# Nine small tiles instead of ten: every large tile moves down by 32 bytes

## The chip, the cores and the metric

The kernel runs on one core of a Trainium2 chip. The metric is the device time of one execution in microseconds (us). Before the change the median of three runs is 1848.85 us, from 1848.84 to 1849.08.

The core has five engines that work side by side: PE (the matrix engine; its weight loads are shown apart, as PEld), DVE (vector), ACT (scalar), POOL (general) and SP (which here issues most of the transfers). Operands lie in an on-chip memory of 128 partitions; an address in this text is a byte offset within a partition and is the same in all 128.

## The reference, cut to what matters

One layer of a streaming encoder on 256 tokens of width 2048, all in float32:

```
x = x + 0.5 * swiglu(rms_norm(x, ffn1_norm), w_gate, w_up, w_down)    # hidden width 5632
h = rms_norm(x, mix_norm);  [u | q | k | v] = h @ w_in                # 4 x 1024 columns
y_ssm = s5_mixer(u)                                                   # diagonal state space, then a gated 1024x1024 product
y_sb  = stick_breaking_attention(rms_norm(q), rms_norm(k), v)         # 8 heads of 128
x = x + concat(rms_norm(y_ssm), rms_norm(y_sb)) @ w_out
x = x + 0.5 * swiglu(rms_norm(x, ffn2_norm), ...)                     # the same again, other weights
gate = sigmoid(rms_norm(x, ple_norm) @ w_ple_gate)
x = x + rms_norm((p @ w_ple_proj) * gate, ple_post_norm)
```

Nearly all arithmetic lies in the products of 256 rows with large weight matrices.

## The kernel before, in words

A product of two float32 matrices is made of three products of a shorter type (`fp32r` in the rows, float32 bits that PE takes in one pass): each operand is split into a part `hi`, a copy rounded to that type, and a rest `lo`; then `hi*hi`, `lo*hi` and `hi*lo` are summed in an accumulator. ACT writes `hi` (line 181), DVE writes `lo` by a subtraction (line 184), and PE runs the three products (lines 323, 324 and 328 in `gemm_half`; lines 495, 496 and 498 in `Seven.product`, which does the feed-forward products with seven block products in place of eight). In each of these the moving operand is a slice of 512 columns of a weight tile (`whi`, `wlo`, or in a second ring `shi`, `slo`), 2048 bytes in each partition, and the stationary operand is a slice of 128 columns of an activation tile (`nhi`, `nlo`, `hhi`, `hlo`), 512 bytes in each partition. Some products are narrower: the gated product of the state-space part (lines 1384, 1388, 1393) has a moving operand of 256 columns, and the attention (lines 1249 to 1295) works with 256 and 512 columns.

Weights come by SP's queue as `raw` tiles of 1 MB (line 313), five buffers deep; `whi` and `wlo` have four buffers each. Where the second ring is there, `weight_pair` (line 284) takes the next pair from it or from the first by a turn of seven, `i % 7 % 2`. The change leaves that turn as it is.

All tiles come from pools, and a pool's tiles are laid one behind the other in the partition. First come a scratch of 1024 bytes for transfers, four small constants, and the pool `const` (`ident`, `ones`, `late_r`, `ident_r`, `tri_r`, `all_r` of 512 bytes each, then `gains` and `rho4`). Then comes the pool `small` with tiles of 8 float32 values, 32 bytes, named `sm`; they hold sums of squares, roots and the like. Behind `small` stand the pools of the large tiles: `wts` (`raw`, `whi`, `wlo`), `act` (`nhi` and so on), `com`, and the pools of the single phases. So the size of `small` sets where every large tile begins, while the constants in front of it don't depend on it.

A tile of `small` is taken by `small()` (line 82); the pool hands its buffers out in turn. A new tile in a buffer waits until the last use of the tile that had this buffer before. The order of instructions on each engine follows from the program's text with the generators that `step()` advances after each half chunk of a product; addresses play no part in it.

Of the kernel before, what the change touches and what calls it, by code (L numbers as in the profile page):

```python
# [33 lines left out]
def layer_kernel(ctx: ExitStack, tc: tile.TileContext, a: dict, shapes: dict, out: bass.AP):  # L34
# [15 lines left out]
    assert TT == 2 and NP == 64 and HC == 16 and DH == P and NC == 64 and SW == NH * DH  # L50

    cpool = ctx.enter_context(tc.tile_pool(name="const", bufs=1))
    smp = ctx.enter_context(tc.tile_pool(name="small", bufs=10))
    wp = ctx.enter_context(tc.tile_pool(name="wts", bufs=4))
    actp = ctx.enter_context(tc.tile_pool(name="act", bufs=1))
    comp = ctx.enter_context(tc.tile_pool(name="com", bufs=1))
# [1620 lines left out]
```

## Time and profile before

| what | value |
|---|---|
| median of three runs | 1848.85 us |
| the profiled execution's own time | 1850.29 us |
| its span, first to last instruction | 1848.5 us |
| PE busy | 1836.6 us, 99% of the span |
| DVE busy | 1462.7 us, 79% |
| ACT busy | 1019.6 us, 55% |
| POOL busy | 62.1 us, 3% |
| granted clock of PE, mean | 0.998 |

The profiled execution took 1.44 us more than the median of the runs, and 1.8 us of its time lie outside the span. A row of a timeline gives the start within the span and the time that the instruction took, both in microseconds, then engine, source line, operation, `out<-in` and how many equal instructions the row merges. The time that a matmul takes includes the run through the array, which overlaps with the next matmul; what a matmul costs in a dense stream is the distance from its start to the next one's start.

### The profile page before, as it was taken

Reading aid. Unit: us, or ns where it says so; the run is one execution under the profiler, and the core shown is the slowest. Engines: PE = TensorE matmul, PEld = TensorE weight load, DVE = VectorE, ACT = ScalarE, POOL = GpSimd, SP = SyncE. Lnnn points to the kernel's source line nnn. Section 1 sums busy time; section 2 is a strip of 40 time slices with the busy share of each in tenths; the row PEclk is TensorE's granted clock in tenths of the full one; section 3 lists DMA queues with packets and bytes.
Section 4 is the critical chain, followed back from the end, with each engine's and each line's share of the span. In section 5 each row is a group of like instructions: output and inputs, shape, how many; then the busy total and the mean of one; then the engine's idle time right before and its main releaser. Section 6 shows DMA issues by size and latency. Waiting matters only on the chain. (4 is left out here: it accounts for less than half of the span.)

```text
span 1848.5 us, 23966 instructions
## 1 busy us (share of the span) xinstructions
PE 1836.6 (99%) x9032; PEld 1519.8 (82%) x9032; DVE 1462.7 (79%) x1718; ACT 1019.6 (55%) x1187; POOL 62.1 (3%) x108
## 2 busy tenths in 40 slices
PE   9999999999999999999999999999999999999998
PEld 7888887888888888888897888888888888888887
DVE  8967664999987975687566799989898998797655
ACT  7444443555565655365685465555555645565554
POOL 0011000000000000010021000000000000000000
PEclk9999999999999999999999999999999999999999
DMA  9888867567657566675636776675656585656563
GB/s 331 286 270 281 251 213 219 182 228 239 227 189 249 191 231 206 192 263 166 212 142 215 219 272 210 227 239 190 205 182 227 198 269 185 247 183 232 180 220 125
DMA packets 232307, 406.36 MB, mean 220 GB/s; under 512 B 26784, under 2 KB 50720, under 8 KB 231904
## 3 DMA queue, kind: packets, MB, share of 16 engines
q1 hardware_dynamic: 227824, 392.81, 63.5%
q0 software_dynamic: 3648, 10.62, 1.8%
q8 instruction: 70, 1.15, 0.3%
q10 hardware_dynamic: 720, 1.41, 0.2%
q14 instruction: 45, 0.37, 0.1%
HBM read 373.46 MB, written 11.93 MB: 208 GB/s over the span
## 5 line engine op out<-in xcount | busy, mean ns | idle before, releaser
L184 DVE TENSOR_TENSOR wlo<-raw,whi 128x1024 fp32r<-128x1024 f32 x473 | 573.2, 1224 | 214.1 <-ACT whi L181 206.5
L181 ACT CAST whi<-raw 128x1024 fp32r<-128x1024 f32 x473 | 491.4, 1050 | 398.3 <-PE acc L324 258.0
L323 PE MATMUL acc<-whi,nhi 128*128 128x512 f32 x1112 | 436.8, 393 | 1.9 <-ACT whi L181 1.6
L324 PE MATMUL acc<-whi,nlo 128*128 128x512 f32 x1112 | 433.7, 390 | 0.0
L328 PE MATMUL acc<-wlo,nhi 128*128 128x512 f32 x1112 | 304.4, 390 | 0.4 <-DVE wlo L184 0.4
L323 PEld LDWEIGHTS acc<-whi,nhi 128*128 128x128 f32 x1112 | 209.2, 188 | 47.9 <-ACT whi L181 3.0
L328 PEld LDWEIGHTS acc<-wlo,nhi 128*128 128x128 f32 x1112 | 208.8, 188 | 44.6 <-DVE wlo L184 1.2
L324 PEld LDWEIGHTS acc<-whi,nlo 128*128 128x128 f32 x1112 | 209.4, 188 | 42.4
L184 DVE TENSOR_TENSOR slo<-raw,shi 128x1024 fp32r<-128x1024 f32 x166 | 202.5, 1220 | 43.8 <-ACT shi L181 43.6
L181 ACT CAST shi<-raw 128x1024 fp32r<-128x1024 f32 x166 | 174.3, 1051 | 113.4 <-PE acc L324 32.7
L181 ACT CAST whi<-sum 128x1024 fp32r<-128x1024 f32 x61 | 64.2, 1052 | 96.1 <-DVE sum L502 80.8
L181 ACT CAST shi<-sum 128x1024 fp32r<-128x1024 f32 x47 | 49.5, 1052 | 74.4 <-DVE sum L502 62.4
L324 PE MATMUL acc<-whi,hlo 128*128 128x512 f32 x216 | 84.1, 389 | 0.0
L323 PE MATMUL acc<-whi,hhi 128*128 128x512 f32 x216 | 84.1, 389 | 0.0
L324 PE MATMUL aux<-whi,hlo 128*128 128x512 f32 x200 | 78.0, 390 | 0.8 <-DVE hlo L184 0.8
L323 PE MATMUL aux<-whi,hhi 128*128 128x512 f32 x200 | 77.8, 389 | 0.0
L184 DVE TENSOR_TENSOR wlo<-sum,whi 128x1024 fp32r<-128x1024 f32 x61 | 74.6, 1222 | 1.9 <-ACT whi L181 1.2
L184 DVE TENSOR_TENSOR hlo<-hT,hhi 128x1024 fp32r<-128x1024 f32 x56 | 68.3, 1219 | 4.8 <-ACT hhi L181 4.5
L502 DVE TENSOR_TENSOR sum<-sum,raw 128x1024 f32<-128x1024 f32 x54 | 66.0, 1222 | 1.0
L181 ACT CAST hhi<-hT 128x1024 fp32r<-128x1024 f32 x56 | 58.6, 1047 | 13.8 <-PE aux L328 11.7
L328 PE MATMUL acc<-wlo,hhi 128*128 128x512 f32 x216 | 65.7, 390 | 0.2 <-DVE wlo L184 0.2
L324 PE MATMUL acc<-shi,hlo 128*128 128x512 f32 x160 | 62.3, 389 | 0.0
(373 smaller groups left out, 3016.9 us busy)
## 6 DMA issues: line engine op xcount, KB each, us to landing
raw<-in_ffn_w_up SPq DMA_DIRECT2D x88, 1024.0 KB, 5.9
raw<-in_ffn_w_down SPq DMA_DIRECT2D x88, 1024.0 KB, 5.1
raw<-in_ffn_w_gate SPq DMA_DIRECT2D x86, 1024.0 KB, 7.1
raw<-in_w_in SPq DMA_DIRECT2D x32, 1024.0 KB, 5.9
raw<-in_w_out SPq DMA_DIRECT2D x16, 1024.0 KB, 5.3
raw<-in_w_ple_gate SPq DMA_DIRECT2D x16, 1024.0 KB, 5.4
hT<-mid SPq DMA_DIRECT2D x160, 64.0 KB, 4.2
h<-mid SPq DMA_DIRECT2D x176, 32.0 KB, 2.8
```

The costliest lines, as they stand in the source:

```text
L181: copy = nc.scalar.copy(hi, src)
L184: nc.vector.tensor_tensor(out=lo, in0=src, in1=hi.bitcast(F32), op=ALU.subtract)
L323: nc.tensor.matmul(ps[t], lhsT=lh, rhs=hi[:, j, cols], start=start and j == 0, stop=False)
L324: nc.tensor.matmul(ps[t], lhsT=ll, rhs=hi[:, j, cols], start=False, stop=False)
L328: nc.tensor.matmul(ps[t], lhsT=lh, rhs=lo[:, j, cols], start=False, stop=stop and j == 1)
L502: nc.vector.tensor_tensor(out=t, in0=x, in1=y, op=ALU.add)
```

## The change

The pool of small tiles has nine buffers instead of ten:

```diff
-    smp = ctx.enter_context(tc.tile_pool(name="small", bufs=10))
+    smp = ctx.enter_context(tc.tile_pool(name="small", bufs=9))
```

The pool shrinks from 320 to 288 bytes, so every tile behind it begins 32 bytes lower. The first `raw` tile began at byte 6112, which is 32 above a multiple of 64; it now begins at 6080, a multiple of 64 (and 64 above a multiple of 128). All other large tiles have sizes that are multiples of 64 and move in the same way: `whi` from 47072 to 47040, `nhi` from 79840 to 79808, and so on. Counted over the built programs, 7990 of the 7998 `fp32r` matmuls had a moving operand that began 32 above a multiple of 64 and 7956 a stationary one; after the change none has. The others read constants: the moving operand `late_r` at line 1249, and the stationary operands `ident_r`, `tri_r` and `all_r` at lines 1249, 1288 to 1295 and 1571, began at multiples of 128 before and still do.

The order of the instructions is the same on all five engines. The small tiles fall on other buffers of their pool. Of all the waits in the program a single one is changed: POOL's instruction at line 1564, near the end, writes to a small tile whose buffer had before been last used by an ACT instruction of the last gate block (line 1495); it now waits for a much earlier ACT instruction (line 598).

## The prediction

> **What bounds the kernel now.** I read the busy times first, then the slices, then what PE waited for, then the distances between matmul starts.
>
> ```profile
> PE 1836.6 (99%) x9032; PEld 1519.8 (82%) x9032; DVE 1462.7 (79%) x1718; ACT 1019.6 (55%) x1187; POOL 62.1 (3%) x108
> ```
>
> PE is busy from end to end. DVE, the next, has 1848.5 - 1462.7 = 386 us to spare. The slices show whether that holds in each stage:
>
> ```profile
> PE   9999999999999999999999999999999999999998
> DVE  8967664999987975687566799989898998797655
> ```
>
> PE is full in all forty. DVE is nearly full in some (slices 8 to 11, most of 24 to 33), so a faster PE would meet DVE there. A busy PE could still be one that waits within its rows, so next comes the list of PE's own waits, all of it:
>
> ```profile
> PE acc L328 <- DVE slo L184: 2.2, 1, 2.2
> PE acc L323 <- ACT whi L181: 1.6, 2, 1.1
> PE aux L248 <- POOL ones L125: 1.1, 1, 1.1
> PE aux L324 <- DVE hlo L184: 0.8, 1, 0.8
> PE acc L328 <- DVE wlo L184: 0.6, 3, 0.2
> PE aux L495 <- ACT whi L181: 0.3, 1, 0.3
> PE acc L323 <- ACT whi L273: 0.2, 1, 0.2
> ```
>
> They come to 6.8 us. Whatever the change does for DVE, ACT or transfers cannot bring more than about that. What is left is PE's own rate. In the chain of work that ended last, six rows of line 328, four matmuls each, come at one distance near the end; the first and the last of the six are
>
> ```profile
> 1743.20 0.91 PE acc L328 x4
> ...
> 1756.80 0.91 PE acc L328 x4
> ```
>
> Between two of them lie twelve matmuls of 512 columns (four of line 323, four of 324, four of 328), so 60 matmuls in 13.60 us: 226.7 ns each. The number of them, from the table of one stretch over the whole span for line 323 and then for line 495 (PE busy and its count stand third and fourth):
>
> ```profile
> 0.00:1848.50 1848.50, 863.87 (x2210) 415.39 (x2210) 1.00 0.66 220
> 0.00:1848.50 1848.50, 147.31 (x378) 70.98 (x378) 1.00 0.66 220
> ```
>
> Lines 324 and 328 have the same count as 323, and 496 and 498 that of 495: 3 x 2210 + 3 x 378 = 7764, twelve of which have 256 columns; with 18 more at lines 1288 and 1571 there are 7770 of 512 columns. 7770 x 226.7 ns = 1761 us of the 1848.5. So each nanosecond on a wide matmul is 7.8 us of the kernel, and 0.5 ns is 0.2%, about what a measurement of this kernel can tell from no change.
>
> The 226.7 ns are not all columns. The gated product has moving operands of 256 columns, fourteen starts from the first of these rows to the last:
>
> ```profile
> 933.21 0.28 PE L1384 MATMUL acc<-hhi,whi 128*128 128x256 f32 x1
> ...
> 934.89 0.28 PE L1384 MATMUL acc<-hhi,whi 128*128 128x256 f32 x1
> ```
>
> 1.68 us / 14 = 120 ns. 256 columns more cost 226.7 - 120 = 106.7 ns, so 512 columns are 213.3 ns and **13.3 ns are a fixed cost of each matmul**: 7770 x 13.3 ns = 104 us. The question is whether this fixed cost has to do with operands that begin 32 bytes above a multiple of 64.
>
> **The change part by part.**
>
> *The start of the moving operand.* One place of the kernel has had it aligned all along: line 1249 in the attention reads `late_r`, a constant at a multiple of 128, with the stationary `ident_r`, also at a multiple of 128. Two of them follow each other; the first and the last time:
>
> ```profile
> 893.28 0.40 PE L1249 MATMUL aux<-late_r,ident_r 128*128 128x256 f32 x2
> 893.51 0.38 PE L1255 MATMUL aux<-q,k 128*128 128x256 f32 x1
> ...
> 938.96 0.40 PE L1249 MATMUL aux<-late_r,ident_r 128*128 128x256 f32 x2
> 939.20 0.59 PE L1255 MATMUL aux<-q,k 128*128 128x256 f32 x2
> ```
>
> From the first start to the start behind the pair: 0.23 and 0.24 us for two, 0.47 / 4 = 117.5 ns each. Nearby stand matmuls of the same width whose moving operands `sph` and `spl` begin 32 above a multiple of 64:
>
> ```profile
> 915.93 0.39 PE L1288 MATMUL aux<-sph,tri_r 128*128 128x512 f32 x1
> 916.16 0.28 PE L1291 MATMUL aux<-sph,all_r 128*128 128x256 f32 x1
> 916.28 0.29 PE L1295 MATMUL aux<-sph,tri_r 128*128 128x256 f32 x1
> 916.40 0.39 PE L1288 MATMUL aux<-spl,tri_r 128*128 128x512 f32 x1
> 916.64 0.28 PE L1291 MATMUL aux<-spl,all_r 128*128 128x256 f32 x1
> 916.76 0.28 PE L1295 MATMUL aux<-spl,tri_r 128*128 128x256 f32 x1
> 916.87 0.40 PE L323 MATMUL acc<-whi,nhi 128*128 128x512 f32 x1
> 917.11 0.39 PE L324 MATMUL acc<-whi,nlo 128*128 128x512 f32 x1
> ```
>
> 916.16 to 916.40 and 916.64 to 916.87: 0.47 / 4 = 117.5 ns. Aligned and unaligned cost the same to the resolution of the rows, some 3 ns. An aligned matmul without the fixed cost would have shown 106.7 ns, a pair 0.21 us. So I take 0 for this part. The comparison is not quite clean: `late_r` is read as the same 128 columns twice, and these are four-fold samples at half width amid a disturbed stream. I keep both ends below.
>
> *The start of the stationary operand.* Weight loads in two rows, with `ident_r` aligned in the first (shortest, median and longest time in ns) and `nhi` unaligned in the second (188 is its mean):
>
> ```profile
> L1249 PEld LDWEIGHTS aux<-late_r,ident_r x8: 187/188/192, 893.0 to 939.0; 128*128 128x128 f32 x8
> L323 PEld LDWEIGHTS acc<-whi,nhi 128*128 128x128 f32 x1112 | 209.2, 188 | 47.9 <-ACT whi L181 3.0
> ```
>
> 188 ns each. I take 0. The end on the slow side comes from line 1288 above, 512 columns with an aligned stationary operand: 916.40 to 916.64 is 0.24 us, 13 ns more than 226.7. But line 323, unaligned, is followed in that same place at the same distance (916.87 to 917.11), so the place is slow, not the alignment.
>
> *DVE, ACT and transfers.* Their operands move too. ACT wrote a constant of 128 columns once from an unaligned tile (`h`) and once from an aligned one (`ones`):
>
> ```profile
> L133 ACT ACTIVATE tri_r<-h x1: 312/312/312, 54.1 to 54.1; 128x128 fp32r<-128x128 f32 x1
> L136 ACT ACTIVATE all_r<-ones x1: 307/307/307, 19.0 to 19.0; 128x128 fp32r<-128x128 f32 x1
> ```
>
> 5 ns, or nothing: one sample each. No row shows DVE or a transfer on aligned large tiles, so they are bounded by who waits for them. If they get faster, the gain is at most PE's 6.8 us of waits. If they get slower, PE's lead over them covers it: DVE's 386 us. I take 0.
>
> *One buffer less.* A shorter turn could put a wait before an instruction. It puts none: the one wait that differs, POOL's at line 1564, is for an earlier ACT instruction than before, and ends with DVE's square in any case:
>
> ```profile
> POOL sm L1564 <- DVE sq L1557: 353.9, 1, 353.9
> ```
>
> Cost 0; the cover is DVE at line 1557, which is in the chain to the end anyway.
>
> **The sum**: 0 + 0 + 0 + 0 on the profiled execution, 1850.29 us, which is 1.44 above the median of the runs; on the median, **1848.9 us**. Own range of this case: 1845.2 to 1852.6, the 0.2%.
>
> **The rivals.**
>
> *Faster by the whole fixed cost.* If each matmul pays 13.3 ns since its rows begin off a boundary, they go, less what a stream keeps in any case. That rest is seen at half speed, where PE's clock was granted at 0.56:
>
> ```profile
> 323.00:326.60 3.60, 3.60 (x11) 2.78 (x10) 3.60 (x6) 1.68 (x2) 0.00 (x0) 0.56 0.84 279
> 325.26 0.63 PE L323 MATMUL acc<-whi,nhi 128*128 128x512 f32 x1
> 325.69 0.63 PE L324 MATMUL acc<-whi,nlo 128*128 128x512 f32 x1
> 326.12 0.63 PE L323 MATMUL acc<-whi,nhi 128*128 128x512 f32 x1
> ```
>
> 0.86 us for two, 430 ns, against 2 x 213.3 = 426.7 for the columns: hardly any fixed cost. It belongs to a limit that shows only at full speed, as reading operands might. That speaks for this rival; line 1249 speaks against it. Price: between 10 and 13.3 ns, say 11.7 x 7770 = 91 us, 1758 us; DVE at 1462.7 us of that is 83%, and its full slices would give some back. Chance 0.06. The Trainium skill, page "TensorE: Matmul & The Clock Gate", section "Back-to-back issue gap", gives the distance of two matmuls at full clock as N / 2.4 + 2.5 ns, 215.8 for 512 columns. The trace differs, 226.7; by the page's figure the sum would be 10.9 x 7770 = 85 us, an estimate, and this rival's time.
>
> *Faster by one piece of 64 bytes.* 2048 bytes that begin at a multiple of 64 touch 32 such pieces, otherwise 33. One piece is 213.3 / 32 = 6.7 ns, half of the fixed cost: 7770 x 6.7 = 52 us, 1797 us. For it: the size fits. Against it: line 1249 again, where a pair would have come in 0.22 us or less; it was 0.23 and 0.24. Chance 0.08. The Trainium skill, page "SBUF — State Buffer", section "Specifications (TRN2)", gives lines of 16 bytes; by it a start at 32 is as good as one at 64, and the sum is 0. No run here shows the size of a line.
>
> *Faster at the edges.* The matmuls stay, and PE's waits shrink: at most 6.8 us, so 1842 to 1845. Chance 0.05.
>
> *Slower: aligned stationary operands.* The 13 ns at line 1288 would be theirs, not the place's. Averaged with 0.23 us for the one before (915.93 to 916.16) it is 8 ns: 65 us, 1914 us. It decides from 0.5 ns on. For it speaks that row; against it that its unaligned neighbour shows the same. Chance 0.05.
>
> *Slower: one more stand of PE with a half clock behind it.* Before 322.46 PE stood 2.2 us for DVE's `slo`, and then ran at half clock: eight distances of about 430 ns, 200 too much each, 1.6 us. If DVE slowed by a few tens of ns where it is full, PE would stand a second and third time, 3.8 us each: 1852.7 to 1856.5. It needs a stand over some 2 us; the next longest in the list is 1.1. Chance 0.06.
>
> *It does not do what it says.* The addresses do move, as the built program shows; this is no rival.
>
> **How the numbers follow.** No change within 0.2%: 1 less the rivals, 0.70. Faster 0.06 + 0.08 + 0.05 = 0.19; slower 0.05 + 0.06 = 0.11. The range takes the likeliest with the two small rivals at its sides, 0.70 + 0.05 + 0.06 = 0.81, so 1841 to 1857; the three large shifts of the rate lie outside.
>
> **What would show it.** Twelve matmuls still come every 2.72 us and pairs of line 1384 every 0.24: the fixed cost stays. 2.64 would be the 64-byte piece, below 2.60 the whole fixed cost. Weight loads stay at 188 ns, the wait at line 1564 still ends with DVE. I am wrong if the distance of wide matmuls moves by over 0.5 ns, and most likely then since line 1249, with its doubled columns, was no fair sample.

## The result and the profile after

The kernel after the change takes 1849.46 us in the median of 14 runs (1848.57 to 1850.25), the kernel before 1849.41 us (14 runs, 1848.84 to 1850.40). The ratio is 1.0000 with a 95% interval from 0.9992 to 1.0008: no difference. The predicted 1848.9 us is 0.6 us below the measured time, which lies inside the range of 1841 to 1857. The 0.6 us lie in the starting point, not in the change: the prediction began from the first three runs of the kernel before (1848.85 us).

The busy times of the profiled execution (its own time 1849.49 us, its span 1847.7 us):

```profile
PE 1835.4 (99%) x9032; PEld 1518.1 (82%) x9032; DVE 1462.3 (79%) x1718; ACT 1019.6 (55%) x1187; POOL 62.1 (3%) x108
```

The rate of the wide matmuls is read again from the chain of work that ended last; the first and the last of six rows:

```profile
1742.39 0.91 PE acc L328 x4
...
1755.99 0.91 PE acc L328 x4
```

60 matmuls in 13.60 us, 226.7 ns each, to the last digit the distance of before. The gated product with 256 columns, twelve starts from the first of these rows to the last:

```profile
932.72 0.28 PE L1388 MATMUL acc<-hlo,whi 128*128 128x256 f32 x1
...
934.16 0.28 PE L1388 MATMUL acc<-hlo,whi 128*128 128x256 f32 x1
```

1.44 us / 12 = 120 ns, as before. From the list of PE's own waits, the longest:

```profile
PE acc L328 <- DVE slo L184: 2.2, 1, 2.2
```

From the list of all engines' waits, POOL's at line 1564:

```profile
POOL sm L1564 <- DVE sq L1557: 353.9, 1, 353.9
```

Both are those of before. PE's own waits come to 7.1 us, against 6.8. The two profiled spans differ by 0.8 us. After PE's stand of 2.2 us the clock had fallen to 0.56 in the profile of before; this time it stayed at full speed there, and 18 matmuls ran in that stretch instead of 11:

```profile
323.00:326.60 3.60, 3.60 (x18) 2.95 (x17) 3.60 (x6) 1.59 (x2) 0.00 (x0) 1.00 0.80 249
```

One place did change. In the attention, line 1288 has 512 columns with the stationary constant `tri_r` at a multiple of 128 and a moving operand that stood 32 above a multiple of 64 and now stands at one:

```profile
915.10 0.39 PE L1288 MATMUL aux<-sph,tri_r 128*128 128x512 f32 x1
915.33 0.28 PE L1291 MATMUL aux<-sph,all_r 128*128 128x256 f32 x1
...
915.56 0.39 PE L1288 MATMUL aux<-spl,tri_r 128*128 128x512 f32 x1
915.79 0.28 PE L1291 MATMUL aux<-spl,all_r 128*128 128x256 f32 x1
```

Two distances of 0.23 us, where before they were 0.23 and 0.24. Line 1288 has eight matmuls in the whole kernel; by the trace's starts in nanoseconds their mean distance fell from 231.9 to 229.4 ns. That is next to nothing, but it became a lead.

### The profile page after: what moved, and what is told of

Its sections match the earlier page's. It is cut to its first block, busy times and chain, and to the rows that moved or that the text cites. A ratio compares the mean times of both kernels' runs of the same rounds, so it can differ in the third digit from the quotient of the medians.

```text
span 1847.7 us, 23966 instructions
## 1 busy us (share of the span) xinstructions
PE 1835.4 (99%) x9032; PEld 1518.1 (82%) x9032; DVE 1462.3 (79%) x1718; ACT 1019.6 (55%) x1187; POOL 62.1 (3%) x108
## 5 line engine op out<-in xcount | busy, mean ns | idle before, releaser
L184 DVE TENSOR_TENSOR wlo<-raw,whi 128x1024 fp32r<-128x1024 f32 x473 | 572.3, 1221 | 215.8 <-ACT whi L181 207.4
L323 PE MATMUL acc<-shi,hhi 128*128 128x512 f32 x160 | 62.3, 389 | 0.0
```

Of the source, the lines that this page charges most:

```text
L184: nc.vector.tensor_tensor(out=lo, in0=src, in1=hi.bitcast(F32), op=ALU.subtract)
L323: nc.tensor.matmul(ps[t], lhsT=lh, rhs=hi[:, j, cols], start=start and j == 0, stop=False)
```

## The experiments

Times are medians, each with the kernel before timed beside it. The diffs show the lines that matter; `...` stands for what lies between them.

**Each half of the change alone.** First ten small tiles as before, with all operands at multiples of 128:

```diff
     smp = ctx.enter_context(tc.tile_pool(name="small", bufs=10))
+    ctx.enter_context(tc.tile_pool(name="pad", bufs=1)).tile([P, 8], F32, name="pad")
...
-    late_r, ident_r, tri_r, all_r = (cpool.tile([P, P], F32R, name=s + "_r") for s in ("late", "ident", "tri", "all"))
+    late_r, ident_r, tri_r = (cpool.tile([P, P], F32R, name=s + "_r") for s in ("late", "ident", "tri"))
...
-        nc.scalar.activation(all_r, ones, AF.Copy, scale=-1.0)
...
+    all_r = pool.tile([P, P], F32R, name="all_r")
+    nc.scalar.activation(all_r, ones, AF.Copy, scale=-1.0)
     attn_scores(pool, (6, 7, 16, 19))
```

> Ten small tiles as before the change, and every wide operand at a multiple of 128 (the constant all_r moved out of the way into the attention's pool, and 32 bytes of filling behind the small tiles). Theory (the start of an operand costs nothing): 1849.4 us as before, within 0.2%, twelve wide matmuls every 2.72 us. Rival (rows are read in pieces of 128 bytes, so that 64 above a multiple of 128 was as bad as 32): twelve matmuls in 2.56 to 2.60 us, 1758 to 1765 us.

Then nine small tiles, with the large tiles back at the addresses of before:

```diff
     smp = ctx.enter_context(tc.tile_pool(name="small", bufs=9))
+    ctx.enter_context(tc.tile_pool(name="pad", bufs=1)).tile([P, 8], F32, name="pad")
```

> Nine small tiles as after the change, with 32 bytes of filling, so that all large tiles stand where they stood before it. Theory (one buffer less puts no wait): 1849.4 us, within 0.2%, the wait at line 1564 ended by DVE's square as before. Rival (the two halves of the change cancel, so that the shorter turn alone costs what the alignment alone wins): slower by more than 3.7 us, with e1 faster by the same.

Measured: 1849.34 us, ratio 0.9995 (0.9986 to 1.0004), and 1850.09 us, ratio 0.9998 (0.9988 to 1.0007). The chain of the first:

```profile
1742.34 0.91 PE acc L328 x4
...
1753.22 0.91 PE acc L328 x4
```

10.88 us over four steps, 2.72 us for twelve. In the second, POOL's wait at what was line 1564 was ended by DVE's square after 353.9 us, as before. So neither half does anything. The change had left operands 64 above a multiple of 128; here they all stood at multiples of 128 and nothing was won, so the rival falls for pieces of 128 bytes too.

**Odd starts of one operand.** To see whether a start can cost at all, nearly all moving operands were put 4 bytes on, then nearly all stationary ones (`all_r` moved as above, for room; in the first run the tiles of `first_quarters` were changed in the same way):

```diff
-        return [
-            pool.tile([P, 2, NB], F32R, tag=s, name=uid(s), bufs=3 if pool is extra else None) for s in tags
+        tiles = [
+            pool.tile([P, 2 * NB + 8], F32R, tag=s, name=uid(s), bufs=3 if pool is extra else None) for s in tags
         ]
+        return [u[:, 1 : 1 + 2 * NB].rearrange("p (j n) -> p j n", j=2) for u in tiles]
```

> Nearly every moving operand begins 4 bytes above a multiple of 32, the stationary ones stay at multiples of 64. Theory (no cost for a start, however odd): 1849.4 us, within 0.2%. Rival (only small pieces matter, such as 16 bytes, and both 32 and 64 were on their boundaries): one more piece of 16 bytes in 128 is 213.3 / 128 = 1.7 ns for each wide matmul, 13 us: 1862 us, and twelve matmuls in 2.74 us; if an odd start halves the rate of reading, far more.

```diff
-            actp.tile([P, 4, T], F32R, tag=kind + s, name=uid(kind + s), bufs={"n": 4, "h": 2}[kind])
+            actp.tile([P, 4 * T + 8], F32R, tag=kind + s, name=uid(kind + s), bufs={"n": 4, "h": 2}[kind])[
+                :, 1 : 1 + 4 * T
+            ].rearrange("p (j t) -> p j t", j=4)
```

> Nearly every stationary operand begins 4 bytes above a multiple of 32, the moving ones stay at multiples of 64. Theory: 1849.4 us, within 0.2%, weight loads at 188 ns. Rival (the fixed cost lies in the weight load and grows with the pieces that it touches, 33 pieces of 16 bytes in place of 32): the fixed 13.3 ns grow by 1/32, 0.4 ns for each wide matmul, 3 us: 1852.6 us; weight loads longer than 188 ns.

Measured: 1922.25 us, ratio 1.0387 (1.0370 to 1.0404), and 1887.58 us, ratio 1.0200 (1.0185 to 1.0215). Both are misses: the theory had no change, the rivals 13 and 3 us, and it was 72 and 37. In the chain of the first, four steps of twelve matmuls:

```profile
1817.13 0.95 PE acc L334 x4
...
1828.53 0.95 PE acc L334 x4
```

11.40 us / 48 = 237.5 ns, 11 ns more on each wide matmul of this stretch. So "no start costs anything" fell, though the change under study costs nothing. The new tiles are also 32 bytes longer, so that the buffers of one tile no longer begin alike; this comes up again below.

**The matmuls by themselves.** A kernel of streams alone, twelve of 36 matmuls each, on two tiles made from `x` that lie 4096 bytes apart; one of the twelve:

```diff
+    for k in range(COUNT):
+        pin(nc.tensor.matmul(ps, lhsT=stat[:, m(k % 4) : m(k % 4) + P], rhs=mov[:, 8 : 8 + N], start=True, stop=True))
```

> Only streams of 36 matmuls each on two tiles made of x, with nothing beside them; the output is x itself, the whole layer is left out. It measures the distance of matmul starts. Theory (no start costs anything): 226.7 ns for 512 columns of fp32r with the moving operand 0, 64, 32 or 4 bytes above a multiple of 128, and with the stationary one 0, 32 or 4 bytes above; 120 ns for 256 columns, both read straight and as the same 128 columns twice. Rival (line 1249 was no fair sample): the straight aligned 256 columns come in 107 to 113 ns and only the doubled ones in 118 to 120; aligned 512 columns below 226.7. On the fixed 13.3 ns: if it belongs to the load of 128 stationary columns, it falls to about 6.7 ns with 64 and 3.3 ns with 32 columns; if it is the same for each matmul, 226.7 ns stays; with bf16 operands, half as many bytes, it is below 13.3 ns if reading bytes sets it.

This kernel and the two more like it below ran once each; at full clock a stream with both starts at 0 came out between 226.6 and 226.8 ns in all three. Mean distances of starts, worked out from the trace's starts without the first four of each stream (starts are counted from the beginning of the tile; the bf16 stream is the first and began at half clock):

| moving operand | stationary operand | ns |
|---|---|---|
| 512 columns at 0 | 0 | 226.8 |
| 512 at 64 bytes | 0 | 228.8 |
| 512 at 32 bytes | 0 | 233.3 |
| 512 at 4 bytes | 0 | 236.5 |
| 512 at 0 | 32 bytes | 233.4 |
| 512 at 0 | 4 bytes | 232.5 |
| 512 at 0 | 0, the same columns each time | 227.3 |
| 512 at 0 | 0, 64 columns | 230.0 |
| 512 at 0 | 0, 32 columns | 231.7 |
| 256 at 0 | 0 | 120.0 |
| the same 128 twice, at 0 | 0 | 120.0 |
| 512 at 0, bf16 | 0, bf16 | 216 (median) |

The doubled columns of line 1249 are a fair sample after all: 120.0 ns both ways. But 32 bytes on one side cost 6.6 ns, and both operands of the kernel before stood 32 bytes above a multiple of 64 at 226.7 ns. Start for start these don't fit together. They would if it were the distance between the two starts that counts.

**Distance or start?** The new theory was tried in the kernel and in a grid. In the kernel, weight tiles stay and activation tiles move by 32 bytes (`all_r` moved as above):

```diff
     wp = ctx.enter_context(tc.tile_pool(name="wts", bufs=4))
+    ctx.enter_context(tc.tile_pool(name="pad", bufs=1)).tile([P, 8], F32, name="pad")
     actp = ctx.enter_context(tc.tile_pool(name="act", bufs=1))
+    ctx.enter_context(tc.tile_pool(name="pad_2", bufs=1)).tile([P, 8], F32, name="pad_2")
     comp = ctx.enter_context(tc.tile_pool(name="com", bufs=1))
```

> The kernel after the change with two fillings of 32 bytes: all weight tiles stay at multiples of 64, all activation tiles stand 32 above one. So the moving and the stationary operand of every wide matmul begin 32 bytes apart (modulo 64), where they began alike before the change and after it. Neither start is new: 32 and 0 were each harmless when both had it. New theory (what counts is the distance of the two starts, not where either lies; the streams gave 233 ns at 32 and 0, 227 at 0 and 0): 226.7 becomes about 233, 6.6 ns x 7770 = 51 us: 1901 us, between 1890 and 1905. Old theory (no multiple of 32 matters): 1849 to 1851 us.

Measured: 1896.37 us, ratio 1.0245 (1.0228 to 1.0262). The chain, four steps of twelve:

```profile
1786.45 0.93 PE acc L329 x4
...
1797.65 0.93 PE acc L329 x4
```

11.20 us / 48 = 233.3 ns, what the stream gave for 32 bytes on one side. Only a distance was made; both starts, at 0 and at 32, had been harmless. The 45 us are a little under the 51 expected, 5.8 ns on the average matmul. By the trace's starts, the dense wide matmuls (distances under 300 ns) took 233.1 ns on average, 6.4 more than after the change and near the 6.6 expected; a part came back, since the longer distances, with PE's waits in them, became fewer (59 in place of 69).

Two rows of this run bear on the prediction. The gated product, with 256 columns, had its operands pushed apart by 32 bytes as well, and it was not slower:

```profile
952.31 0.28 PE L1385 MATMUL acc<-hhi,whi 128*128 128x256 f32 x1
...
953.71 0.28 PE L1385 MATMUL acc<-hhi,whi 128*128 128x256 f32 x1
```

1.40 us / 12 = 116.7 ns, against 120; over the whole product the mean distance is 117.6 ns against 120.7. So of the two widths only 512 columns paid for this distance.

The grid had 34 streams, one for each pair of starts, such as this one:

```diff
+    run("m8_s8_26", 8, 8, lambda ps, l, r: nc.tensor.matmul(ps, lhsT=l, rhs=r, start=True, stop=True))
```

> Only streams of 32 matmuls of 512 columns, one for each pair of starts (in elements of 4 bytes) of the moving and the stationary operand; the layer is left out and the output is x. New theory (the distance counts): with both at 1, 4, 8, 16 or 24 elements 226.7 ns, as with both at 0; with the moving one alone at 8 elements 233 ns and at 1 element 236 to 237; with 8 and 24 (apart by 16) as with 16 and 0, 229 ns. Rival (each start off a multiple of 16 elements costs for itself): both at 1 or both at 8 cost at least as much as one alone, 233 ns and more. Of special use would be a pair below 226.7 ns; neither theory expects one.

Here are the timeline rows of some streams of 32 matmuls. From the start of one to the start of the next is its time; the names give the starts of moving and stationary operand in elements of 4 bytes, in order 32 and 0, 64 and 0, 128 and 0, 0 and 1 (lines 46 to 49), then 1 and 1, 4 and 4, 8 and 8, 16 and 16, 24 and 24, 8 and 24, 24 and 8 (lines 57 to 63):

```profile
108.32 7.62 PE L46 MATMUL m_s<-mov,stat 128*128 128x512 f32 x32
115.78 7.44 PE L47 MATMUL m_s<-mov,stat 128*128 128x512 f32 x32
123.06 7.42 PE L48 MATMUL m_s<-mov,stat 128*128 128x512 f32 x32
130.32 7.60 PE L49 MATMUL m_s<-mov,stat 128*128 128x512 f32 x32
...
189.79 7.76 PE L57 MATMUL m_s<-mov,stat 128*128 128x512 f32 x32
197.39 7.55 PE L58 MATMUL m_s<-mov,stat 128*128 128x512 f32 x32
204.78 7.44 PE L59 MATMUL m_s<-mov,stat 128*128 128x512 f32 x32
212.06 7.45 PE L60 MATMUL m_s<-mov,stat 128*128 128x512 f32 x32
219.35 7.44 PE L61 MATMUL m_s<-mov,stat 128*128 128x512 f32 x32
226.63 7.63 PE L62 MATMUL m_s<-mov,stat 128*128 128x512 f32 x32
234.10 7.63 PE L63 MATMUL m_s<-mov,stat 128*128 128x512 f32 x32
```

7.26 to 7.29 us, that is 226.7 to 227.1 ns once the change of stream is left out, for distances of 64 and 128 elements (256 and 512 bytes) and for both operands at 8, 16 or 24 elements. 7.46 and 7.47 us, 233 ns, for 32 and 0, that is 128 bytes apart with both at a multiple of 128, and for 8 and 24. 7.60 us, 238 ns, for both at 1 element, and 7.39 us, 231 ns, for both at 4: below 32 bytes a start costs for itself as well, so that the theory of distance alone missed there. Its 229 ns for 8 and 24 were a miss too. And the stream of 24 and 8, 16 elements apart, took 233 ns by the trace's starts, where 16 and 0 took 229: for unequal starts the distance alone is not the rule at multiples of 32 bytes either.

**128 and 256 bytes in the kernel.** The grid says that 256 bytes bring the operands together again, while 128 bytes don't, although every operand then begins at a multiple of 64. The edit is that of the run at 32 bytes, with both fillings of 32 or of 64 elements in place of 8; the first of them:

```diff
-    ctx.enter_context(tc.tile_pool(name="pad", bufs=1)).tile([P, 8], F32, name="pad")
+    ctx.enter_context(tc.tile_pool(name="pad", bufs=1)).tile([P, 32], F32, name="pad")
```

> The kernel after the change with two fillings of 128 bytes: every operand still begins at a multiple of 64, the moving and the stationary operand of nearly every wide matmul 128 bytes apart modulo 256. Theory (the distance counts, in pieces of 256 bytes; the grid gave 233.1 ns at a distance of 128 bytes): as with 32 bytes, 1895 to 1901 us, twelve wide matmuls in 2.78 to 2.80 us. Rival (the distance counts only below 64 bytes, and operands at multiples of 64 are fine): 1849 to 1851 us.

> The same with fillings of 256 bytes: the two operands begin at equal places modulo 256, though no longer modulo 512. Theory (distance modulo 256; the grid gave 226.7 ns at 256 and 512 bytes): 1849 to 1851 us, as the kernel before. Rival (any shift of the activation tiles against the weight tiles costs, for some other reason): 1895 us as with 32 and 128.

Measured: 1891.69 us at 128 bytes, ratio 1.0223 (1.0207 to 1.0238), and 1849.96 us at 256, ratio 0.9998 (0.9988 to 1.0008). The chain for 128 bytes, three steps of twelve:

```profile
1782.31 0.93 PE acc L329 x4
...
1790.71 0.93 PE acc L329 x4
```

The chain for 256 bytes, three steps as well:

```profile
1742.54 0.91 PE acc L329 x4
...
1750.70 0.91 PE acc L329 x4
```

8.40 us / 36 = 233.3 ns, and 8.16 us / 36 = 226.7 ns. The rates were those of the theory, and both rivals fell. The time at 128 bytes, 41 us over the kernel before, is 3 us below the range that had been expected: over the whole kernel the dense wide matmuls took 232.5 ns on average, less than in these rows.

**Is there anything below 226.7?** Streams of 24 with the moving operand at every start from 0 to 64 elements and the stationary one at 0, and other widths; two of the streams:

```diff
+    run("m5_s0_6", 5, 0, lambda ps, l, r: nc.tensor.matmul(ps, lhsT=l, rhs=r, start=True, stop=True))
+    run("n384", 0, 0, lambda ps, l, r: nc.tensor.matmul(ps[:, :384], lhsT=l, rhs=r[:, :384], start=True, stop=True))
```

> Streams of 24 matmuls of 512 columns for every start of the moving operand from 0 to 64 elements, the stationary one at 0, then streams of 64 to 448 columns with both at 0; the layer is left out. Theory: 226.7 ns is the floor, at 0 and 64 elements; between 228 and 238 elsewhere. If some distance were below 226.7, a faster kernel could be built on it. On the fixed cost: 106.7 + 13.3 = 120 at 256 columns and 173 at 384 if it is the same for every width; if the load of 128 stationary columns is a floor, the streams of 64 and 128 columns stay near one value.

Distances of 5, 6 and 7 elements (lines 39 to 41), then widths of 320 and 384 columns (lines 104 and 105):

```profile
44.37 5.92 PE L39 MATMUL m_s<-mov,stat 128*128 128x512 f32 x24
50.12 5.77 PE L40 MATMUL m_s<-mov,stat 128*128 128x512 f32 x24
55.73 5.60 PE L41 MATMUL m_s<-mov,stat 128*128 128x512 f32 x24
61.17 5.76 PE L42 MATMUL m_s<-mov,stat 128*128 128x512 f32 x24
...
400.87 3.69 PE L104 MATMUL n<-mov,stat 128*128 128x320 f32 x24
404.39 4.33 PE L105 MATMUL n<-mov,stat 128*128 128x384 f32 x24
408.56 5.11 PE L106 MATMUL n<-mov,stat 128*128 128x448 f32 x24
```

5.75, 5.61 and 5.44 us over 24: 240, 234 and 226.7 ns. None of the 65 starts is below 226.7; it is reached at 0 and 64, but also at 7, 15, 39, 59, 60 and 63 elements, and the others lie between 228 and 240 without a plain order. The expectation, 226.7 at 0 and 64 only and at most 238 elsewhere, was a miss in both. For 512 columns the kernel before was thus at the lowest rate of all starts tried, and none of them makes it faster. The fixed cost is 13.3 ns at 256, 320, 384 and 512 columns and 20 at 448 (206.7 ns). Streams of 64 and of 128 columns both took 112 ns while the clock was full, as the expectation had it for a floor set by the weight load; that it is the load is not shown. (The granted clock was 0.50 for 10 us in the streams of 128, 192 and 256 columns; there all three took 213 ns. The 120 ns for 256 columns are from the first streams.)

These streams also explain the run with the odd moving operands. Counted over its built program, the two operands of its wide matmuls were nearly all 1, 9, 17 and so on to 57 elements apart. The streams at these distances took 234.7 to 240.0 ns, 236.6 when weighted by the counts, and the dense wide matmuls of that run took 236.5 on average. So its 72 us need no cost of a start for itself. For the odd stationary operands the same sum gives 228.6 ns and the run had 231.8: there the start costs something for itself as well.

## Why the prediction was right

*The sum of zeros* was right, and each term of it: wide matmuls at 226.7 ns, weight loads near 188, the wait at line 1564 unchanged, DVE, ACT and transfers without effect on PE. Each half of the change alone gave the same. The reason given for the first two zeros, that starts don't count, was too wide, though. They came out at zero because both operands of nearly every wide matmul move by the same 32 bytes, and the prediction did not say so. That much was luck.

*The start of the moving operand.* Line 1249 was read rightly. The doubt about its doubled columns was not needed: straight and doubled columns both take 120.0 ns. What it could show was narrower than I took it for, though. It compared operands at equal places with others 96 bytes apart, but at 256 columns, and at 256 columns a distance of 32 bytes did not slow the gated product either. It did not show that starts don't count at 512 columns, which two runs refuted with 37 and 72 us.

*The start of the stationary operand.* Here one reading failed, without moving the sum. I put the slow rows of line 1288 down to the place, since an unaligned neighbour was slow too. By the addresses of the built programs `sph` and `tri_r` began 96 bytes apart (modulo 256) before the change, 64 after it and 128 in the run with all operands at multiples of 128. The eight matmuls took 231.9, 229.4 and 233.1 ns on average; the streams at these distances took 233.3, 228.9 and 233.5. The ten matmuls of line 1571, at the same 96 and 64 bytes, went from 232.5 to 228.5 (their first distance, over 600 ns, left out). So the distance was at least part of it. The place was slow besides: line 323 behind it, with equal starts, took 236 ns before it settled. The rows, rounded to 10 ns, made the difference 8 ns where it was 5. The rival built on that row, slower by 65 us through aligned stationary operands, had the wrong cause: what costs is one operand moved against the other, 45 us for 32 bytes. It did not come about since the change moves both. Counted over the built programs, 7964 of the 7998 `fp32r` matmuls had starts at equal places modulo 256 bytes before, and the same 7964 after: all large tiles lie behind `small` and have sizes that keep this, so a shift of the whole leaves every distance as it was. That was in the addresses, and I did not look at distances.

*The rival at the edges.* PE's own waits did not shrink; they came to 7.1 us in place of 6.8.

*The fast rivals.* Neither pieces of 64 nor of 128 bytes carry the fixed cost: with all operands at multiples of 128 the distance was 226.7 ns. What the 13.3 ns are stays open. No start that was tried lowers them at 512 columns. They don't fall with fewer stationary columns (230 and 232 ns with 64 and 32) or with the same ones again (227). With bf16 they are 2.5 ns, by the last twenty distances of that stream (215.8 on average). That is the 215.8 ns which the Trainium skill, page "TensorE: Matmul & The Clock Gate", section "Back-to-back issue gap", gives for 512 columns; it holds here for bf16 and not for fp32r. A bf16 operand has half the bytes, but a cost for each byte of the moving operand would grow with the columns, and from 256 to 512 this one does not. At half clock it is gone (427 ns for 512 columns). Why, no run shows.

*The slow rival with the clock.* No second stand came. The stand of 2.2 us was there in both profiles, with the half clock behind it in one and not in the other, so its length alone does not decide that. Runs of the kernel before have mean clocks from 0.998 to 1.000, so the half clock comes and goes without the change. Whether the change makes it rarer the runs don't show.

## What to carry to other kernels

Before an edit that shifts addresses is costed, compare not only where the operands of the bounding instruction begin, but how far the two begin from each other; a shift that moves both alike changes nothing. For fp32r matmuls of 512 columns, starts equal modulo 256 bytes (and at multiples of 32) gave 226.7 to 227.1 ns, and most other pairs tried gave 228 to 240: in this kernel 32 bytes of filling between two pools cost 45 us. So the distance is worth checking whenever a pool in between changes its size. A comparison at another width does not settle it: at 256 columns the same 32 bytes cost nothing.

## What was not expected of the hardware

The rate of a matmul depends on where its two operands begin against each other. The Trainium skill, page "TensorE: Matmul & The Clock Gate", section "Step-by-step: what each phase is for", says that loading the next stationary tile doesn't take reading bandwidth from the running matmul, since both have ports of their own. In these runs the place of the one against the other changes the distance of two matmuls of 512 columns by 6.7 ns at 32 and at 128 bytes, up to 13 ns at 20 bytes, and by nothing at 256 bytes. Whether the two reads get in each other's way, or how else that comes about, the runs don't show. A start at 16 bytes for both operands costs 4 ns against one at 32, where the lines of 16 bytes that the Trainium skill, page "SBUF — State Buffer", section "Specifications (TRN2)", gives would have made them alike.
